# Masked softmax on one core: stores whole and held back, four loads in flight

## The chip, the cores and the metric

The kernel runs on one core of a Trainium2 chip. The metric is the device time of one execution in microseconds (us). The kernel before took 155.86 us, the median of three runs (155.79 to 156.03).

The core has five engines, each with its own queue of instructions: TensorE (PE), VectorE (DVE), ScalarE (ACT), GpSimd (POOL) and SyncE (SP). They wait for one another only through semaphores. Data goes between the chip's main memory (DRAM here) and the on-chip memory SBUF through 16 DMA engines, which all queues share. SBUF has 128 partitions.

## What is computed

A softmax along the last axis of x (16 batches, 8 heads, 256 x 256, float32), where batch b counts only its first lengths[b] columns; the other columns of the result are zero.

```python
def reference(x, lengths):
    batch, heads, seq_q, seq_k = x.shape
    result = np.zeros_like(x)
    for b in range(batch):
        length = lengths[b]
        masked = x[b, :, :, :length].copy()
        masked = masked - np.max(masked, axis=-1, keepdims=True)
        exp_masked = np.exp(masked)
        result[b, :, :, :length] = exp_masked / np.sum(exp_masked, axis=-1, keepdims=True)
    return result
```

The lengths are drawn between 128 and 255. With the draw used here they are 188, 233, 229, 243, 195, 252, 165, 210, 222, 180, 209, 157, 159, 199, 214, 248.

## The kernel before

One batch is 2048 rows of 256 numbers, 2 MB. It is laid over the 128 partitions so that each partition holds 16 whole rows (nt = 16), 16 KB that also lie together in DRAM. SBUF has room for 8 batches (`xt`, 8 slots); batch b uses slot b % 8.

**Loads.** The first four batches (ahead = 4) are loaded whole by SP at the start: batch 0 in two halves (L109), batches 1 to 3 in one transfer each (L111). Their landing raises `s_ld`: s_ld[0] and s_ld[1] for the halves of batch 0, s_ld[b+1] for batch b. Batches 4 to 15 are loaded by POOL in a loop (L153): it reads the length (L156), and a tree of branches (`pick`, L126) issues the transfer of the smallest sufficient width, 160 to 240 columns in steps of 8, or all 256 (L130). Such a narrow load moves only the left part of each row. What stands in the right part of the slot is old or was set to zero (L149), and the mask covers it. Two loads are in flight: load n waits for load n-2 (`s_sw`, one semaphore for even and one for odd batches, L158) and for the store of batch n-8, whose slot it takes (`s_st`, L159). The first load also waits for s_ld[3], the landing of batch 2 (L152).

**Compute.** For each batch VectorE first masks (L195): columns from the length on get a very large negative number. ScalarE then takes the exponential of each of the 16 rows of a partition, with the row's sum as a side result (L252), in two halves of 8 rows. VectorE divides each half by the sums (L219, L222); the end of a half raises `s_out`. VectorE's order is fixed: for batches 4 and on it is first half of b, mask of b+1, second half of b; for batches 1 to 3 the mask of b+1 comes first.

**Stores.** SP issues the stores (L120), in order of the batches. `parts` (L50) says how a batch is cut: whole for batches 0, 13 and 14, in a half and two quarters for 1 to 7, in two halves for 8 to 12 and 15. A part goes as soon as its half is divided (L117), and the first part of a batch also waits until the store of batch b-2 has landed (L119). The cut sets the size of a packet: a quarter has 4 KB per partition, a half 8 KB, a whole batch 16 KB. `s_st` counts 64 for a batch, 16 for each quarter.

SP's queue thus holds loads of batches 0 to 3 and then all stores. POOL's queue holds the loads of batches 4 to 15. On the DMA side they are two queues: q1 (hardware) for what SP issues, q0 (software) for what POOL issues.

Of the kernel before, what the change touches and what calls it, by code (L numbers as in the profile page):

```python
# [16 lines left out]
POOL = mybir.EngineType.Pool  # L17
# [3 lines left out]
def kernel(  # L21
# [6 lines left out]
    nc = tc.nc  # L28
    P = nc.NUM_PARTITIONS

    batch, heads, seq_q, seq_k = x.shape
    rows = heads * seq_q
    assert rows % P == 0
    nt = rows // P
    half = nt // 2
    quarter = nt // 4

    x_f = x.rearrange("b h q k -> b (h q) k").rearrange("b (p t) k -> b p t k", p=P)
    out_f = out.rearrange("b h q k -> b (h q) k").rearrange("b (p t) k -> b p t k", p=P)

    slots = 8
    ahead = 4
    assert slots - ahead == 4 and batch % slots == 0

    widths = list(range(160, 248, 8))
# [1 line left out]
    mid = seq_k // 2  # L47
    big = 1.0e30

    def parts(b):  # L50


        if b == 0:
            cuts = [0, nt]
        elif b < 8:
            cuts = [0, half, half + quarter, nt]
        elif b < 13 or b == batch - 1:
            cuts = [0, half, nt]
        else:
            cuts = [0, nt]  # L60
        return [slice(i, j) for i, j in zip(cuts, cuts[1:])]

    pool = ctx.enter_context(tc.tile_pool(name="all", bufs=1))
    psum = ctx.enter_context(tc.tile_pool(name="psum", bufs=1, space=bass.MemoryType.PSUM))
    xt = pool.tile([P, slots, nt, seq_k], F32, name="xt")
# [11 lines left out]
    seed = pool.tile([1, 2], F32, name="seed")  # L77

    sem = lambda n: ctx.enter_context(nc.semaphore(n))
    s_st = [sem("s_st0"), sem("s_st1")]  # L80
    with tc.tile_critical(no_gpsimd_drain=True):  # L81
# [3 lines left out]
        s_lenf = sem("s_lenf")  # L85
        s_ld = [sem(f"s_ld{k}") for k in range(ahead + 1)]

        s_sw = [sem("s_sw0"), sem("s_sw1")]

        s_iota = sem("s_iota")  # L90
        s_fill = sem("s_fill")
# [2 lines left out]
        s_exp = sem("s_exp")  # L94
        s_out = sem("s_out")

        def length(engine, at):

            return nc.values_load(  # L99
                at,  # L100
                engines=[engine],
                skip_runtime_bounds_check_because="compared with constants, never an address",
            )
# [3 lines left out]
        for h in range(2):  # L107
            s = slice(h * half, (h + 1) * half)
# [1 line left out]
        for b in range(1, ahead):  # L110
            nc.sync.dma_start(out=xt[:, b], in_=x_f[b]).then_inc(s_ld[b + 1], 16)  # L111

        nc.sync.wait_ge(s_exp, 3)
        for b in range(batch):
            s_b = s_st[b % 2]
            for s in parts(b):
                nc.sync.wait_ge(s_out, 2 * b + (s.stop - 1) // half + 1)  # L117
                if b >= 2 and s.start == 0:
                    nc.sync.wait_ge(s_b, 64 * (b // 2 + 1))  # L119
                nc.sync.dma_start(  # L120
                    out=out_f[b, :, s, :], in_=xt[:, b % slots, s, :]
                ).then_inc(s_b, 16 * ((s.stop - s.start) // quarter))

        def pick(v, n, slot, par, ws):  # L126

            if len(ws) == 1:
                w = ws[0]
                nc.gpsimd.dma_start(  # L130
                    out=xt[:, slot, :, :w], in_=x_n[:, n, :, :w]
                ).then_inc(s_sw[par], 16)
                return
            m = (len(ws) - 1) // 2
            with nc.gpsimd.If(v <= ws[m]):  # L135
                pick(v, n, slot, par, ws[: m + 1])
            with nc.gpsimd.Else():
                pick(v, n, slot, par, ws[m + 1 :])

        x_n = x_f.rearrange("b p t c -> p b t c")  # L140
        nc.gpsimd.iota(  # L141
# [1 line left out]
        ).then_inc(s_iota, 1)  # L143
        nc.gpsimd.memset(ones, 1.0).then_inc(s_ones, 1)  # L144
        for par in range(2):
            nc.gpsimd.memset(seed[:, par : par + 1], 0.0).then_inc(s_st[par], 64)  # L146
        nc.gpsimd.wait_ge(s_v, 2)
        for b in range(ahead, slots):
            nc.gpsimd.memset(xt[:, b, :, low:], 0.0).then_inc(s_fill, 1)  # L149
        nc.gpsimd.wait_ge(s_word, 16)  # L150
        nc.gpsimd.wait_ge(s_fill, slots - ahead)
        nc.gpsimd.wait_ge(s_ld[ahead - 1], 16)  # L152
        with nc.Fori(0, (batch - ahead) // 2, 1, engines=[POOL]) as q:  # L153
            for par in range(2):
                n = 2 * q + (ahead + par)
                v_len = length(POOL, word[0:1, bass.ds(2 * n, 1)])  # L156
                with nc.gpsimd.If(q >= 1):
                    nc.gpsimd.wait_ge(s_sw[par], 16 * q)  # L158
                    nc.gpsimd.wait_ge(s_st[par], 64 * q)  # L159
                pick(v_len, bass.ds(n, 1), bass.ds(n % slots, 1), par, widths + [seq_k])  # L160


        nc.tensor.wait_ge(s_ones, 1)
# [4 lines left out]
        v = 0  # L168

        def step(ins):  # L170
# [8 lines left out]
                out=down, in0=iota_i, scalar1=0.5, scalar2=-big, op0=ALU.add, op1=ALU.mult  # L179
# [7 lines left out]
                out=len_s, in0=len_f, scalar1=big, scalar2=None, op0=ALU.mult  # L187
# [4 lines left out]
        def clip(b, s, lo, hi):  # L192

            t = xt[:, b % slots, s, lo:hi]
            return nc.vector.scalar_tensor_tensor(  # L195
                out=t,
                in0=down[:, None, lo:hi].to_broadcast([P, s.stop - s.start, hi - lo]),
                scalar=len_s[:, b : b + 1],
                in1=t,
                op0=ALU.add,  # L200
                op1=ALU.min,
            )

        def mask(b, s):
            v_len = length(DVE, word[0:1, 2 * b : 2 * b + 1])
            if b == 0:
                nc.vector.wait_ge(s_ld[s.start // half], 16)
            elif b < ahead:
                nc.vector.wait_ge(s_ld[b + 1], 16)
            else:  # L210
                nc.vector.wait_ge(s_sw[b % 2], 16 * ((b - ahead) // 2 + 1))
            with nc.vector.If(v_len < mid):  # L212
                clip(b, s, 0, mid)
            clip(b, s, mid, seq_k).then_inc(s_min, (s.stop - s.start) // half)

        def divide(b, h):
# [10 lines left out]
            ).then_inc(s_out, 1)  # L227

        mask(0, slice(0, half))
        mask(0, slice(half, nt))  # L230
        for b in range(batch):


            first = b == 0 or b >= ahead
            if first:
                divide(b, 0)
            if b + 1 < batch:
                mask(b + 1, slice(0, nt))
            if not first:
                divide(b, 0)  # L240
            divide(b, 1)
# [5 lines left out]
        with nc.Fori(0, 2 * batch, 1, engines=[ACT]) as i:  # L247
            nc.scalar.wait_ge(s_min, i + 1)
            at = bass.ds(i % (2 * slots), 1)
            for j in range(half):  # L250
                e = x_h[:, at, j, :]
                ins = nc.scalar.activation(  # L252
                    out=e, in_=e, func=EXP, accum_out=sum_h[:, bass.ds(i, 1), j]
# [3 lines left out]

    with tc.tile_critical(no_gpsimd_drain=True):
        for par in range(2):
            nc.sync.wait_ge(s_st[par], 64 * (batch // 2 + 1))  # L260


# [28 lines left out]
```

## Time and profile before

| | |
|---|---|
| median of three runs | 155.86 us |
| span of the profiled execution | 154.7 us |
| VectorE busy | 115.7 us (75%) |
| ScalarE busy | 105.2 us (68%) |
| GpSimd busy | 19.0 us (12%) |
| read from DRAM | 28.51 MB |
| written to DRAM | 33.55 MB |
| mean DMA rate over the span | 401 GB/s |
| divide of half a batch (L222) | 32 x 2292 ns |
| masks (L195) | 17 instructions, 37.8 us |
| load issued by POOL to its landing | 13.3 to 20.5 us |
| stores issued by SP | 36: 14 of 512 KB, 19 of 1 MB, 3 of 2 MB |

The span is what the profile shows of one execution; the time of a run is a little longer. "Busy" adds up an engine's own instructions. In the strips of the page the span is cut into 40 equal slices of 3.87 us, and a digit is the busy share of a slice in tenths. In the listing of DMA queues the columns are packets, MB, and the time that the packets took as a share of 16 engines over the stretch. A line of waits says which engine's line waited for what: us in total, times, longest. A line in order of time gives the start, the duration, the engine, the line and what it writes and reads; the number in brackets is the idle time just before.

### The profile page before, as it was taken

To read this page: it belongs to the slowest core of one execution; us is meant where nothing else is said; L and a number is where in the kernel's file an instruction comes from. 1 tells how busy PE (TensorE), PEld (TensorE's weight loads), DVE (VectorE), ACT (ScalarE), POOL (GpSimd) and SP (SyncE) were. 2 spreads that over 40 slices of the span, in tenths; PEclk is the share of its full clock that TensorE was granted. 3 is DMA by queue.
4 is the path that set the end of the run, shared out by engine and by line. 5 is a ranking of instruction groups with operands and counts; after the bars stand their busy time and mean duration, and the time that the engine had idled before them with its cause. 6 is when DMAs were issued, how large, how long until landed. Compare 5 with 4: busy or idle time off the path is not lost.

```text
span 154.7 us, 1324 instructions
## 1 busy us (share of the span) xinstructions
PE 0.2 (0%) x1; PEld 0.1 (0%) x1; DVE 115.7 (75%) x84; ACT 105.2 (68%) x514; POOL 19.0 (12%) x25
## 2 busy tenths in 40 slices
PE   0000000000000000000000000000000000000000
PEld 0000000000000000000000000000000000000000
DVE  1249999952999696979979696969689629796700
ACT  3087799992692959778695959595976906959200
POOL 4910031000220110201111020202001000000000
DMA  4999999999999999999999999999999999999992
GB/s 116 426 449 424 428 398 406 398 407 447 400 410 395 402 409 414 415 417 411 404 424 407 417 408 409 415 416 416 416 417 419 419 448 415 426 445 419 430 421 85
DMA packets 9988, 62.08 MB, mean 401 GB/s; under 512 B 850, under 2 KB 946, under 8 KB 6274
## 3 DMA queue, kind: packets, MB, share of 16 engines
q1 hardware_dynamic: 5904, 41.95, 65.8%
q0 software_dynamic: 4080, 20.12, 32.1%
q14 instruction: 2, 0.02, 0.0%
q10 hardware_dynamic: 2, 0.00, 0.0%
HBM read 28.51 MB, written 33.55 MB: 401 GB/s over the span
## 4 chain that ended last, share of the span: by engine, by line
DMA 55%; DVE 19%; ACT 8%; issue 8%; ACTq 2%; SPq 1%; POOLq 1%; DVEq 0%
DMA xt<-in_x_dram 34%; DMA out_dram<-xt 21%; DVE xt L222 9%; DVE xt L195 9%; ACT xt L252 8%; ACTq L252 2%; DVE inv_sum L219 1%; SPq L109 1%; POOLq L99 0%; SPq L111 0%; SPq L120 0%; DVEq L212 0%; POOLq L135 0%; POOLq L130 0%; ACTq L247 0%
## 5 line engine op out<-in xcount | busy, mean ns | idle before, releaser
L252 ACT ACTIVATE xt<-xt x256 | 102.4, 401 | 37.2 <-DVE xt L195 37.2
L222 DVE TENSOR_TENSOR xt<-xt,inv_sum 128x2048 f32<-128x2048 f32 x32 | 73.4, 2292 | 1.1
L252 ACT ACTIVATION_READ_ACCUMULATOR xt<-xt x256 | 47.9, 187 | 0.0
L195 DVE SCALAR_TENSOR_TENSOR xt<-down,len_s,xt 128x2048 f32<-128x2048 f32 (+1 forms) x17 | 37.8, 2222 | 13.1 <-DMA xt<-in_x_dram 13.0
L130 POOL DMA_DIRECT2D xt<-in_x_dram x12 | 12.8, 1064 | 95.5 <-issue 50.6
L219 DVE RECIPROCAL inv_sum<-row_sum 128x8 f32<-128x8 f32 x32 | 6.3, 198 | 14.4 <-ACT xt L252 14.4
L149 POOL MEMSET xt<- 128x1536 f32 x4 | 5.3, 1386 | 1.1 <-DVE len_s L186 1.1
L244 ACT ACT_TABLE_LOAD x1 | 1.3, 1283 | 1.6 <-SPq L81 1.6
L178 DVE TENSOR_SCALAR down<-iota_i 128x256 f32<-128x256 int32 x1 | 0.3, 297 | 1.6 <-POOL iota_i L141 1.6
L183 DVE CAST len_b<-word 1x16 bf16<-1x16 int32 x1 | 0.2, 163 | 0.4 <-DMA word<-in_lengths_dram 0.4
L186 DVE TENSOR_SCALAR len_s<-len_f 128x16 f32<-128x16 f32 x1 | 0.2, 174 | 0.3 <-PE len_f L165 0.3
L141 POOL IOTA iota_i<- 128x256 int32 x1 | 0.3, 331 | 0.6 <-SPq L81 0.6
L146 POOL MEMSET seed<- 1x1 f32 x2 | 0.3, 162 | 0.0
L244 ACT ACTIVATE warm<-const-float32-0.0 128x1 f32<-128x1 f32 x1 | 0.2, 203 | 0.0
L144 POOL MEMSET ones<- 1x128 bf16 x1 | 0.2, 194 | 0.0
L165 PE MATMUL len_f<-len_b,ones 1*128 1x16 bf16 x1 | 0.2, 164 | 2.6 <-DVE len_b L183 2.6
L275 POOL MEMSET const-float32-0.0<- 128x1 f32 x1 | 0.1, 98 | 0.3 <-issue 0.3
L165 PEld LDWEIGHTS len_f<-len_b,ones 1*128 1x128 bf16 x1 | 0.1, 99 | 2.6 <-POOL ones L144 2.6
L275 POOL MEMSET const-float32-1.0<- 128x1 f32 x1 | 0.1, 98 | 0.0
L275 POOL MEMSET const-bfloat16-1.0<- 128x1 bf16 x1 | 0.1, 98 | 0.0
L275 POOL MEMSET const-uint8-127<- 128x1 uint8 x1 | 0.1, 98 | 0.0
L275 POOL BASE_LOAD x1 | 0.0, 17 | 0.1
## 6 DMA issues: line engine op xcount, KB each, us to landing
out_dram<-xt SPq DMA_DIRECT2D x19, 1024.0 KB
out_dram<-xt SPq DMA_DIRECT2D x14, 512.0 KB
xt<-in_x_dram SPq DMA_DIRECT2D x3, 2048.0 KB, 16.1
out_dram<-xt SPq DMA_DIRECT2D x3, 2048.0 KB
xt<-in_x_dram POOLq DMA_DIRECT2D x3, 1728.0 KB, 16.9
xt<-in_x_dram POOLq DMA_DIRECT2D x2, 2048.0 KB, 18.5
xt<-in_x_dram POOLq DMA_DIRECT2D x2, 1600.0 KB, 16.8
xt<-in_x_dram POOLq DMA_DIRECT2D x2, 1280.0 KB, 14.8
```

The costliest lines, as they stand in the source:

```text
L109: nc.sync.dma_start(out=xt[:, 0, s], in_=x_f[0, :, s]).then_inc(s_ld[h], 16)
L130: nc.gpsimd.dma_start(out=xt[:, slot, :, :w], in_=x_n[:, n, :, :w]).then_inc(s_sw[par], 16)
L141: nc.gpsimd.iota(iota_i, pattern=[[1, seq_k]], base=0, channel_multiplier=0).then_inc(s_iota, 1)
L146: nc.gpsimd.memset(seed[:, par : par + 1], 0.0).then_inc(s_st[par], 64)
L149: nc.gpsimd.memset(xt[:, b, :, low:], 0.0).then_inc(s_fill, 1)
L165: nc.tensor.matmul(len_f, lhsT=ones, rhs=len_b, start=True, stop=True).then_inc(s_lenf, 1)
L195: return nc.vector.scalar_tensor_tensor(out=t, in0=down[:, None, lo:hi].to_broadcast([P, s.stop - s.start, hi - lo]), scalar=len_s[:, b : ...
L219: step(nc.vector.reciprocal(out=inv_sum[:, b, s], in_=row_sum[:, b, s]))
L222: nc.vector.tensor_tensor(out=t, in0=t, in1=inv_sum[:, b, s, None].to_broadcast([P, half, seq_k]), op=ALU.mult,).then_inc(s_out, 1)
L244: nc.scalar.activation(out=warm, in_=nc.const_aps.tensor(0.0, (P, 1), F32), func=EXP)
L252: ins = nc.scalar.activation(out=e, in_=e, func=EXP, accum_out=sum_h[:, bass.ds(i, 1), j])
L275: nc = _bacc.Bacc("TRN2", target_bir_lowering=False, num_devices=1)
```

## The change

Every batch is stored whole, in one transfer with 16 KB per partition; `parts` is gone. The store of batch b waits for both halves of its batch, for the store of batch b-2, and, up to batch 11, for the landing of the load of batch b+4. `s_st` counts 16 for a batch.

POOL's loads have four semaphores (lead = 4) in place of two. Load n waits for load n-4 and for the store of batch n-8. The loop runs three times over four loads. The first load waits for s_ld[2], the landing of batch 1; this wait stands inside the loop under a branch that only the first turn takes. SP's wait for the third half's exponential (L113) is gone. VectorE's mask waits on the new semaphores; its instructions and those of ScalarE are the same and in the same order.

```diff
-    def parts(b):
-
-
-        if b == 0:
-            cuts = [0, nt]
-        elif b < 8:
-            cuts = [0, half, half + quarter, nt]
-        elif b < 13 or b == batch - 1:
-            cuts = [0, half, nt]
-        else:
-            cuts = [0, nt]
-        return [slice(i, j) for i, j in zip(cuts, cuts[1:])]
+    lead = 4
+    waves = (batch - ahead) // lead
+    assert waves * lead == batch - ahead
...
-        s_sw = [sem("s_sw0"), sem("s_sw1")]
+        s_sw = [sem(f"s_sw{k}") for k in range(lead)]
...
-        nc.sync.wait_ge(s_exp, 3)
         for b in range(batch):
             s_b = s_st[b % 2]
-            for s in parts(b):
-                nc.sync.wait_ge(s_out, 2 * b + (s.stop - 1) // half + 1)
-                if b >= 2 and s.start == 0:
-                    nc.sync.wait_ge(s_b, 64 * (b // 2 + 1))
-                nc.sync.dma_start(
-                    out=out_f[b, :, s, :], in_=xt[:, b % slots, s, :]
-                ).then_inc(s_b, 16 * ((s.stop - s.start) // quarter))
+            nc.sync.wait_ge(s_out, 2 * b + 2)
+            if b + lead < batch:
+                nc.sync.wait_ge(s_sw[b % lead], 16 * (b // lead + 1))
+            if b >= 2:
+                nc.sync.wait_ge(s_b, 16 * (b // 2 + 1))
+            nc.sync.dma_start(out=out_f[b], in_=xt[:, b % slots]).then_inc(s_b, 16)
...
-            nc.gpsimd.memset(seed[:, par : par + 1], 0.0).then_inc(s_st[par], 64)
+            nc.gpsimd.memset(seed[:, par : par + 1], 0.0).then_inc(s_st[par], 16)
...
-        nc.gpsimd.wait_ge(s_ld[ahead - 1], 16)
-        with nc.Fori(0, (batch - ahead) // 2, 1, engines=[POOL]) as q:
-            for par in range(2):
-                n = 2 * q + (ahead + par)
+        with nc.Fori(0, waves, 1, engines=[POOL]) as q:
+            for k in range(lead):
+                n = lead * q + (ahead + k)
                 v_len = length(POOL, word[0:1, bass.ds(2 * n, 1)])
+                if k == 0:
+                    with nc.gpsimd.If(q < 1):
+                        nc.gpsimd.wait_ge(s_ld[2], 16)
                 with nc.gpsimd.If(q >= 1):
-                    nc.gpsimd.wait_ge(s_sw[par], 16 * q)
-                    nc.gpsimd.wait_ge(s_st[par], 64 * q)
-                pick(v_len, bass.ds(n, 1), bass.ds(n % slots, 1), par, widths + [seq_k])
+                    nc.gpsimd.wait_ge(s_sw[k], 16 * q)
+                    nc.gpsimd.wait_ge(s_st[k % 2], 32 * q + 16 * (k // 2))
+                pick(v_len, bass.ds(n, 1), bass.ds(n % slots, 1), k, widths + [seq_k])
...
-                nc.vector.wait_ge(s_sw[b % 2], 16 * ((b - ahead) // 2 + 1))
+                k = b - ahead
+                nc.vector.wait_ge(s_sw[k % lead], 16 * (k // lead + 1))
...
-            nc.sync.wait_ge(s_st[par], 64 * (batch // 2 + 1))
+            nc.sync.wait_ge(s_st[par], 16 * (batch // 2 + 1))
```

More of the change, by code (lines that the diff above doesn't have):

```diff
@@ L35 @@
     half = nt // 2
-    quarter = nt // 4
     x_f = x.rearrange("b h q k -> b (h q) k").rearrange("b (p t) k -> b p t k", p=P)
@@ L111, with pick @@
             nc.sync.dma_start(out=xt[:, b], in_=x_f[b]).then_inc(s_ld[b + 1], 16)
-        nc.sync.wait_ge(s_exp, 3)
         for b in range(batch):
             s_b = s_st[b % 2]
-            for s in parts(b):
-                nc.sync.wait_ge(s_out, 2 * b + (s.stop - 1) // half + 1)
-                if b >= 2 and s.start == 0:
-                    nc.sync.wait_ge(s_b, 64 * (b // 2 + 1))
-                nc.sync.dma_start(
-                    out=out_f[b, :, s, :], in_=xt[:, b % slots, s, :]
-                ).then_inc(s_b, 16 * ((s.stop - s.start) // quarter))
-        def pick(v, n, slot, par, ws):
+            nc.sync.wait_ge(s_out, 2 * b + 2)
[4 more added lines that the diff above has]
+            nc.sync.dma_start(out=out_f[b], in_=xt[:, b % slots]).then_inc(s_b, 16)
+        def pick(v, n, slot, k, ws):
             if len(ws) == 1:
@@ L131, in pick @@
                     out=xt[:, slot, :, :w], in_=x_n[:, n, :, :w]
-                ).then_inc(s_sw[par], 16)
+                ).then_inc(s_sw[k], 16)
                 return
@@ L135, in pick @@
             with nc.gpsimd.If(v <= ws[m]):
-                pick(v, n, slot, par, ws[: m + 1])
+                pick(v, n, slot, k, ws[: m + 1])
             with nc.gpsimd.Else():
-                pick(v, n, slot, par, ws[m + 1 :])
+                pick(v, n, slot, k, ws[m + 1 :])
         x_n = x_f.rearrange("b p t c -> p b t c")
```

## The prediction

> **What bounds the kernel now.** I read the page first, then the waits of the engines and of SP's queue, then what the DMA queues carried in chosen stretches, and last VectorE in order of time. In the page, the strip of DMA shares and the two data queues:
>
> ```profile
> span 154.7 us, 1324 instructions
> DMA  4999999999999999999999999999999999999992
> q1 hardware_dynamic: 5904, 41.95, 65.8%
> q0 software_dynamic: 4080, 20.12, 32.1%
> ```
>
> The 16 DMA engines are full from the second slice to the last but one. 65.8% + 32.1% = 97.9% of 154.7 us is 151.5 us of packets per engine; the 3.2 us that are left lie before the first packet (first load issued at 1.13 us) and after the last. The chain that ended last also hops from transfer to transfer. So the time is the packet time of one DMA engine plus 3.2 us, as long as it never runs dry, and compute is a second bound below it:
>
> ```profile
> DVE xt L195 <- DMA xt<-in_x_dram: 13.0, 5, 4.4
> ...
> SPq L119 <- DMA out_dram<-xt: 92.3, 14, 9.7
> ```
>
> VectorE waited 13.0 us for loads; SP's queue waited 92.3 us for earlier stores: finished batches lay ready and had no DMA. The price of a packet comes from stretches in which q1 carries stores of one size (columns: packets, MB, share of 16 engines). In this order: 16 KB alone (139 to 146.5 us), 8 KB beside narrow loads (112 to 125), 8 KB alone (148 to 150.5), 4 KB beside narrow loads (74.3 to 78.2 and 93.1 to 96.4):
>
> ```profile
> q1 hardware_dynamic: 217, 3.19, 99.5%
> ...
> q1 hardware_dynamic: 486, 3.49, 64.4%
> q0 software_dynamic: 483, 1.97, 37.7%
> ...
> q1 hardware_dynamic: 147, 1.07, 101.6%
> ...
> q1 hardware_dynamic: 221, 0.85, 54.6%
> ...
> q1 hardware_dynamic: 192, 0.71, 54.1%
> ```
>
> Share times 16 times the stretch, over MB, is engine time per MB: 0.995x16x7.5/3.19 = 37.4 us; 0.644x16x13/3.49 = 38.4; 1.016x16x2.5/1.07 = 38.0; 4 KB 40.1 (0.546x16x3.9/0.85) and 40.2. Narrow loads: 0.377x16x13/1.97 = 39.8. The small semaphore packets are in these figures.
>
> **The change part by part.**
>
> 1. Stores whole. Taken away: 14 stores of 512 KB (7.34 MB), 19 of 1 MB (19.92 MB) and 3 of 2 MB (6.29 MB), in 4, 8 and 16 KB packets: 7.34x40.1 + 19.92x38.4 + 6.29x37.4 = 294 + 765 + 235 = 1294 us of engine time, 80.9 us on each of 16. Added: 33.55 MB in 16 KB packets, 33.55x37.4/16 = 78.4 us. Gain 2.5 us. A 16 KB store beside narrow loads is not seen undisturbed. The 8 KB rows show a surcharge of 38.4 over 38.0, 1%; on the 11 stores that can meet loads (23.07 MB) that is 23.07x37.4x0.01/16 = 0.6 us, so 1.9 at the low end. A worse bound, the stretch from 21 to 28 us, is a rival below. I take 2.2 us, midway. SP also issues 20 instructions fewer (374 ns each), hidden under its 92.3 us of waiting.
>
> 2. Holding store b for load b+4 moves bytes and adds none. SP's queue holds only stores at that point, so behind the wait stand later stores, and behind those POOL's loads (load n waits for store n-8). Store 0, issued at 19.86 us, must now wait for load 4. What fills DMA from 19.9 on: loads 2 and 3 are in flight until about 24 (3.3 + the 20.6 us that the slowest of L111's loads took), and load 4 must follow them. POOL is now released by batch 1, which landed at 2.05 + 11.7 = 13.8 us, instead of batch 2. Before, 18.66 to 20.85 us lay between landing and issue, so load 4 is issued at about 16.1. From there to the first packets can be slow: of the load issued at 20.85 only 0.09 MB had moved by 28 us:
>
> ```profile
> DMA packets 194, 2.69 MB, mean 384 GB/s; under 512 B 16, under 2 KB 16, under 8 KB 35
> ...
> q1 hardware_dynamic: 174, 2.59, 94.6%
> q0 software_dynamic: 19, 0.09, 3.2%
> ```
>
> 19 packets on 16 engines mean a start near 27, a lag of some 6 us. So load 4 flows from about 22, before 24: cost zero, and 2 us of cover. Loads 5 to 7 follow at the 3.2 us between POOL's first two issues (20.85 and 24.04), under 4 us of engine time each. Load 4 (1.64 MB, 39.8x1.64/16 = 4.1 us) lands near 28, against 37.4 before (20.85 + 16.54).
>
> 3. Four loads in flight. By the waits, a load is issued when a store ends and a store when a load lands: four transfers are always under way, each batch a load and a store in turn. One batch is 151.5/16 = 9.5 us of engine time. A turn's dead time is 2.2 + 6 us for a load and 0.4 + 1.4 for a store (first load: issued 1.13, first piece of transfer in the chain at 2.51), 10 us. Four batches give 4x9.5 = 38 us of work per turn; 9.5 + 10 of it is a batch's own, so 18 us of queueing cover the dead time. Cost zero; without this cover each microsecond of dry queue is one of span. POOL runs one more branch (on q) in each turn of its loop, three in all, under the same cover.
>
> 4. Compute. Its rows do not change: per batch two L222 of 2.29, one L195 of 2.35, steps of 8.4 us when not starved. What ends the run after the last load (the mask of batch 15 and its last divide):
>
> ```profile
> 134.97 2.34 DVE L195 SCALAR_TENSOR_TENSOR xt<-down,len_s,xt 128x2048 f32<-128x2048 f32 x1
> ...
> 144.33 2.29 DVE L222 TENSOR_TENSOR xt<-xt,inv_sum 128x2048 f32<-128x2048 f32 x1
> ```
>
> Mask 15 to the last divide's end is 11.7 us. The last store used to leave as two halves; whole, it needs 0.4 + 1.4 + 2.10x37.4/16 = 6.7 us after it. So compute alone ends DMA at mask 15 + 18.4 us. DMA's own end will be near 153.4 - 2.2 = 151.2, so mask 15 must start by 132.8. It will: when load 15 lands, the hold lets at most stores 0 to 10 have moved, with all loads 28.51 + 23.07 = 51.6 of 62.1 MB. At the even pace of 151 us for all, that is 2.6 + 0.83x151 = 128 us. By VectorE's own pace: mask 4 started at 37.62 after 4.42 us idle, now 33.2; 9.6 us to mask 5 (47.21) as before, then ten steps of 8.4 (126.58 to 134.97 is one): 126.8. The later, 128, leaves 4.8 us. Hence the tail costs nothing; without the hold it would (the second rival).
>
> Sum: 154.7 - 2.2 = 152.5 us of profiled span. The profiled execution stands 1.2 us below the median of 155.86, so 155.86 - 2.2 = 153.66; I say 153.6.
>
> **The rivals.**
>
> Slower: 16 KB packets are slow beside the software queue. In the stretch 21 to 28 us, the only one where a 16 KB store meets POOL's loads, q1 took 0.946x16x7/2.59 = 40.9 us per MB, not 37.4. If all 23.07 MB of stores 0 to 10 pay that, +3.5x23.07/16 = 5.0 us, net 2.8 slower than before: 158.7. It decides from 37.4 + 2.5x16/23.07 = 39.1 us per MB on. For it: that row. Against: nearly no narrow data moved there, the whole loads of that stretch were hit as well, it began with POOL's very first issue, and a 16 KB load beside 8 KB stores (127 to 133 us) takes 0.6x16x6/1.54 = 37.4:
>
> ```profile
> q0 software_dynamic: 108, 1.54, 60.0%
> q1 hardware_dynamic: 140, 1.02, 40.1%
> ```
>
> I read it as a start-up cost that stays, moved. Chance 0.10.
>
> No change: loads are starved by big store packets. With 8 KB stores the loads' share was 37.7 to 64.4; packets alternate, some 4.4 KB (1.97 MB in 483 packets, the small ones off) at 39.8 us per MB, 175 ns, to 8 KB at 38.4, 315 ns. Against 613 ns they get 22% while stores are queued. If load 15 then comes as late as before, mask 15 at 134.97 gives DMA's end at 153.4 and a time of 155.9; each microsecond past that costs one. Against it: the hold empties the store queue whenever loads fall behind. Chance 0.06.
> The Trainium skill (DMA: Bandwidth & Descriptors, section "Queues, rings and completion order") says that each engine goes round its queues and changes only at the end of a packet; by it, bigger store packets take from the loads. The 37.7 to 64.4 of the trace agrees with it.
>
> A dry queue. If the lag of load 4 is 10 us and not 6, DMA stands from 24 to 26, and a slow first turn may add as much: 2 to 4 us, 155.6 to 157.6. For it: the slow first load. Against: the 2 us of cover, and the 18 in part 3. Chance 0.06.
>
> The change not doing what it says: POOL may not get four loads out at once, as the trace never shows more than two. Then the third simply follows the first's landing, the queue is still fed, and the time is the forecast's.
>
> **How the numbers follow.** Forecast 0.75, rivals 0.10, 0.06, 0.06, and 0.03 for what I do not see. The forecast's own range is 152.4 to 154.6 (a gain of 3.5 to 1.3, for the rounding of the rows, 0.7% on the smallest, and a little dry time). The range of 8 in 10 goes on to 156.4 to take in the no-change rival and the short dry queue. A measurement here tells a difference from none at about 0.2%, 0.3 us. Faster: 0.75 and 0.03 from mild rivals, 0.78; same 0.07; slower 0.15.
>
> **What would show it.** Right: 16 stores of 2048 KB; the two queues' shares sum to near 149.3 us; DMA strip full throughout; 37.4 to 37.8 us per MB of store beside loads; SP's queue waiting for loads; load 4 landing near 28, the wait of 4.42 at batch 4 gone; mask 15 near 128 or before. Wrong: slices of DMA below 9 around 24 to 30 us or at the end (dry); 39 us per MB or more (slow packets); mask 15 past 133 with VectorE waiting for loads (starved).

## The result and the profile after

The changed kernel takes 158.58 us (158.54 to 158.68, 4 runs) against 155.92 for the kernel before in the same runs: slower by 1.6%, ratio 1.0159 with a 95% interval of 1.0144 to 1.0174. The forecast was 153.6 us, in a range of 152.4 to 156.4.

The page of the profile after, with span, DMA strip and data queues (packets, MB, share of 16 engines over the span):

```profile
span 157.1 us, 1298 instructions
DMA  4999999999999999999999999999999999999991
GB/s 115 434 436 434 432 391 358 434 362 414 415 407 365 413 422 421 394 318 416 428 425 387 406 419 421 421 332 421 402 427 449 417 442 421 430 438 417 438 426 67
q1 hardware_dynamic: 3024, 41.94, 63.4%
q0 software_dynamic: 4080, 20.12, 34.1%
```

DMA is still full in every slice but the first and the last, so nothing ran dry for long. But in five slices the rate falls to 318 to 365 GB/s. In the kernel before it was 395 or more in all but the first and the last:

```profile
GB/s 116 426 449 424 428 398 406 398 407 447 400 410 395 402 409 414 415 417 411 404 424 407 417 408 409 415 416 416 416 417 419 419 448 415 426 445 419 430 421 85
```

By queue, in engine time: q1 (whole loads and stores) went from 65.8% of 154.7 to 63.4% of 157.1, 101.8 to 99.6 us: 2.2 us less, the gain that was forecast. q0 (the narrow loads) went from 32.1% of 154.7 to 34.1% of 157.1, 49.7 to 53.6 us: 3.9 us more for the same bytes in the same packets. That is +1.7 us of the +2.4 us of span; the other 0.7 us is, by the same shares, time outside the packets (3.2 us before, 3.9 now).

Where q0 became dearer shows in what the queues carried in short stretches of the changed kernel. In this order: 25 to 28 us, 68 to 71, 85 to 88, and for comparison 60 to 63, and 126 to 146 for stores by themselves:

```profile
q0 software_dynamic: 201, 1.15, 107.5%
...
q0 software_dynamic: 250, 0.98, 102.3%
...
q0 software_dynamic: 266, 1.09, 101.5%
...
q1 hardware_dynamic: 62, 1.02, 79.3%
q0 software_dynamic: 62, 0.26, 21.5%
...
q1 hardware_dynamic: 587, 8.57, 100.2%
```

In the first three no store moves, and narrow loads have the DMA to themselves. They cost 1.075x16x3/1.15 = 44.9 us of engine time per MB, then 50.1 and 44.7 (25 to 28 us holds some packets of the wide load 5 too, which are cheaper). A share can pass 100% where packets overlap or reach over an edge; by bytes alone the three moved 382, 328 and 362 GB/s, the fourth 426. From 60 to 63 us stores run beside them: 0.215x16x3/0.26 = 39.7, the price of the trace before. The stores cost 37.3 there and 37.4 alone. The fourth stretch also shows how the queues share: 62 packets each.
The Trainium skill (DMA: Bandwidth & Descriptors, section "Queues, rings and completion order") has the engines go round the queues packet by packet; the 62 to 62 agrees.

Counted in slices of 1 us, 11.15 of the 20.12 MB of loads moved in slices in which q1 had less than 15% of the engines, at 44.5 us per MB; the rest cost 40.0. That is 11.15x4.5/16 = 3.1 of the 3.9 us. In the kernel before there is one such slice, with 0.33 MB.

VectorE at batch 4 and at batch 15, and its and SP's waits:

```profile
33.59 2.34 DVE L183 SCALAR_TENSOR_TENSOR xt<-down,len_s,xt 128x2048 f32<-128x2048 f32 x1
...
130.51 2.35 DVE L183 SCALAR_TENSOR_TENSOR xt<-down,len_s,xt 128x2048 f32<-128x2048 f32 x1
```

```profile
DVE xt L183 <- DMA xt<-in_x_dram: 8.6, 5, 3.6
...
SPq L109 <- DMA xt<-in_x_dram: 88.3, 10, 13.8
SPq L107 <- DMA xt<-in_x_dram: 31.5, 2, 25.8
```

Batch 4 no longer waits (4.42 us before), mask 15 starts at 130.5 in place of 135.0, and SP waits for loads, which is the hold (L107; L109 is the next wait, and the list names what came last). The schedule thus did what was worked out, and the price of a narrow load did not stay what it was.

### The profile page after: what moved, and what is told of

Same layout as the page of the kernel before. It is cut to its first block, busy times and chain, and to the rows that moved or that the text cites. A ratio compares the mean times of both kernels' runs of the same rounds, so it can differ in the third digit from the quotient of the medians.

```text
span 157.1 us, 1298 instructions
## 1 busy us (share of the span) xinstructions
PE 0.2 (0%) x1; PEld 0.1 (0%) x1; DVE 115.6 (74%) x84; ACT 105.2 (67%) x514; POOL 19.0 (12%) x25
## 3 DMA queue, kind: packets, MB, share of 16 engines
q1 hardware_dynamic: 3024, 41.94, 63.4%
q0 software_dynamic: 4080, 20.12, 34.1%
## 4 chain that ended last, share of the span: by engine, by line
DMA 71%; issue 6%; DVE 5%; ACT 4%; POOLq 2%; ACTq 1%; SPq 1%; POOL 0%; DVEq 0%
DMA xt<-in_x_dram 57%; DMA out_dram<-xt 14%; ACT xt L241 4%; DVE xt L183 3%; DVE xt L211 2%; ACTq L241 1%; SPq L99 1%; POOLq L121 0%; POOLq L116 0%; POOL xt L116 0%; POOLq L89 0%; DVE inv_sum L208 0%; POOLq L145 0%; POOLq L123 0%; ACTq L236 0%
## 5 line engine op out<-in xcount | busy, mean ns | idle before, releaser
L241 ACT ACTIVATE xt<-xt x256 | 102.3, 401 | 32.8 <-DVE xt L183 32.8
L183 DVE SCALAR_TENSOR_TENSOR xt<-down,len_s,xt 128x2048 f32<-128x2048 f32 (+1 forms) x17 | 37.8, 2222 | 8.7 <-DMA xt<-in_x_dram 8.6
## 6 DMA issues: line engine op xcount, KB each, us to landing
xt<-in_x_dram SPq DMA_DIRECT2D x3, 2048.0 KB, 16.1
```

The lines of the kernel that those rows point to most:

```text
L183: return nc.vector.scalar_tensor_tensor(out=t, in0=down[:, None, lo:hi].to_broadcast([P, s.stop - s.start, hi - lo]), scalar=len_s[:, b : ...
L241: ins = nc.scalar.activation(out=e, in_=e, func=EXP, accum_out=sum_h[:, bass.ds(i, 1), j])
```

## The experiments

Ratios are to the kernel before in the same runs, with 95% intervals. "q0" is the software queue's time per engine, its share times the span. The last column is what q0 moved without stores: MB in slices of 1 us in which q1 had less than 15% of the engines.

| run | stores | hold | loads in flight, released by | time us | ratio | q0 us | without stores, MB |
|---|---|---|---|---|---|---|---|
| before | cut | no | 2, batch 2 | 155.92 | 1 | 49.7 | 0.3 |
| changed | whole | yes | 4, batch 1 | 158.58 | 1.0159 (1.0144 to 1.0174) | 53.6 | 11.2 |
| e1_no_hold | whole | no | 4, batch 1 | 162.38 | 1.0408 (1.0391 to 1.0426) | 53.0 | 8.2 |
| e2_two_loads | whole | yes | 2, batch 1 | 158.86 | 1.0183 (1.0166 to 1.0200) | 54.1 | 13.6 |
| f2_whole_before | whole | no | 2, batch 2 | 162.24 | 1.0405 (1.0377 to 1.0432) | 53.8 | 9.6 |
| f1_halves_held | halves | yes | 4, batch 1 | 157.11 | 1.0059 (1.0043 to 1.0075) | 51.3 | 5.3 |
| f5_cuts_held | cut | yes | 4, batch 1 | 156.38 | 1.0016 (1.0006 to 1.0026) | 50.6 | 3.5 |
| f4_early_four | cut | no | 4, batch 1 | 157.03 | 1.0056 (1.0036 to 1.0076) | 50.0 | 0 |
| g4_four_late | cut | no | 4, batch 2 | 156.54 | 1.0033 (1.0018 to 1.0047) | 49.7 | 0 |
| g3_before_held | cut | yes | 2, batch 2 | 157.45 | 1.0096 (1.0072 to 1.0119) | 51.5 | 4.2 |

**Without the hold.** `e1_no_hold`:

```diff
-            if b + lead < batch:
-                nc.sync.wait_ge(s_sw[b % lead], 16 * (b // lead + 1))
```

> The changed kernel without the wait of store b for load b+4. In the changed kernel a narrow load cost 46 us of engine time per MB in stretches where no store was queued (68 to 71 us: 0.98 MB, 102.3% of 16 engines x 3 us, is 50) and 40 beside stores. Theory A (a narrow load alone in the DMA is slow, and the hold makes such stretches): without the hold stores are queued nearly always, the software queue's time falls from 53.6 us per engine (34.1% of 157.1) to about 50, and the packet time of both queues to 149.5 us; but the loads lose their lead, so mask 15 starts at 134 us or later and the time is 155 to 158. Theory B (four loads in the software queue at once are slow, whatever else runs): the queue's time stays near 53.6 us also beside stores, time 158 or more. Theory C (the waits let DMA run dry, prices do not matter): software queue's time stays at 53 to 54 us.

It took 162.38 us, and q0 stayed at 32.8% of 161.6 us, 53.0. Theory A missed twice: the stretches without stores do not need the hold, and the time was worse than its range. From 84 to 87 us of this run only loads moved, at 1.027x16x3/1.04 = 47.4 us per MB:

```profile
q0 software_dynamic: 266, 1.04, 102.7%
```

By its numbers the run fits theories B and C; the next runs are against them. What the hold had been worth is seen at the end, in VectorE's waits, its mask of batch 15 and the DMA strip of this run:

```profile
DVE xt L181 <- DMA xt<-in_x_dram: 19.9, 10, 4.9
...
142.45 2.35 DVE L181 SCALAR_TENSOR_TENSOR xt<-down,len_s,xt 128x2048 f32<-128x2048 f32 x1 [1.23 <-DMA xt<-in_x_dram]
```

```profile
DMA  4999999999999999999999999999999999974774
```

Mask 15 starts at 142.5, and the DMA stands partly idle in the last slices while compute catches up. Loads starved by big store packets, which the prediction had as a rival, are real; the hold is what keeps them off.

**Two loads in flight.** `e2_two_loads`; a load waits for the load two before it:

```diff
...
-                    nc.gpsimd.wait_ge(s_sw[k], 16 * q)
+                    nc.gpsimd.wait_ge(s_sw[(k + 2) % lead], 16 * q + 16 * (k // 2))
```

> The changed kernel, hold kept, but a load also waits for the load two before it, so that two are in flight as in the kernel before. Theory A: the hold still leaves stretches without stores, narrow loads there still cost 45 us per MB or more, the software queue keeps 52 us per engine or more, time 157 to 160. Theory B: with two in flight the price is 40 everywhere, the software queue's time is 50 us per engine, time 154 to 155.5.

It took 158.86 us with q0 at 54.1: the changed kernel over again. Four loads in flight are not what costs (theory B falls).

**Full loads.** `e3_wide_held` is the changed kernel, `e4_wide_before` the kernel before, both with 256 columns in every load:

```diff
-                pick(..., widths + [seq_k])
+                pick(..., [seq_k])
```

> The changed kernel with every load at the full 256 columns: 16 KB packets in the loads too, 25.17 MB in place of 20.12 from the software queue. At 37.4 us per MB that is 58.8 us per engine, 5.2 more than the 53.6 of the changed kernel and 9.1 more than the 49.7 of the kernel before. Theory A: 16 KB packets do not care whether they are alone, so the loss is gone and only the cheaper stores remain: 158.6 + 5.2 = 163.8 or a little under, 1 to 2.5 us faster than the kernel before with full loads. Theory B and C: the order of the two stays as it was, this one slower by 1 to 3 us than the kernel before with full loads.

> The kernel before with every load at the full 256 columns: 9.1 us more of packet time, so 155.9 + 9.1 = 165.0 us by all theories (its share of loads beside 4 and 8 KB stores grows, which may let the last load land earlier). It is the base for the run before.

They took 164.75 and 165.95 us (ratios to before 1.0561, 1.0544 to 1.0579, and 1.0635, 1.0615 to 1.0656). Each took about 1 us more than expected. With loads in 16 KB packets the changed schedule wins by 1.2 us, about half of the 2.2 that had been forecast. The waits are the same here, so the loss belongs to the narrow loads, and not to the waits. What is missing of the gain is on q0, 60.0 us in e3 and 59.0 in e4. It shows in e3 from 30 to 33.5 us, around the start of the first store, where 0.82 MB of full loads took 84.8% of the engines, 57.9 us per MB. From 27 to 30 us, also without stores, they cost 37.7; what happens at 30 stays open.

**Only part of the change.** Whole stores alone on the kernel before (`f2_whole_before`: `parts` gives `[0, nt]` for every batch); halves in place of whole stores in the changed kernel (`f1_halves_held`); the old cuts in the changed kernel (`f5_cuts_held`); the same without the hold (`f4_early_four`). The core of f1:

```diff
-            nc.sync.dma_start(out=out_f[b], in_=xt[:, b % slots]).then_inc(s_b, 16)
+            for h in range(2):
+                s = slice(h * half, (h + 1) * half)
...
+                nc.sync.dma_start(
+                    out=out_f[b, :, s, :], in_=xt[:, b % slots, s, :]
+                ).then_inc(s_b, 16)
```

> The kernel before with whole stores and nothing else: no hold, two loads in flight. Theory A: the 16 KB packets alone make the stretches without stores; narrow loads 43 us per MB or more, and the last mask comes later than 135 us for want of the hold: 159 to 163. Theory D: no hold, no loss; the cheaper stores show, 153.5 to 155.

> The changed kernel with each store in two halves of 8 KB packets, hold and four loads in flight kept. Theory A now in this form: what decides is whether store packets last beside the loads. A batch needs 54 parts of store to 46 of load; with 16 KB packets stores take 78% while they are queued, run out, and leave narrow loads alone at 46 us per MB; with 8 KB they take 64%, so fewer loads run alone. Expected: narrow loads in all 40 to 42 us per MB (43.7 in the changed kernel), stores 38.4 (37.7), packet time 99.6 + 2 and 53.6 - 2 to 4, time 155.5 to 158. Theory D (the hold itself costs, since it waits for the slowest of the 16 engines): the time stays at 158.6 or goes up by the 2 us of the smaller packets, 160.5.

> The kernel before with its cuts of the stores and no hold, but four loads in flight, released by batch 1. By theory A nothing changes in the packets (stores of 4 and 8 KB still last beside the loads): narrow loads 40 us per MB, time 155 to 156.5. By theory B (four in flight cost) it would be 157 or more.

> The changed kernel with the old cuts of the stores (halves and quarters), hold and four loads in flight kept. Theory A: with 4 KB packets stores take 48% while loads are queued and the hold is what runs them dry, little; narrow loads at 40 to 41.5, stores at 38.6, time 155 to 157. Theory D: 157.5 to 160.

f1, f2 and f5 fell into theory A's ranges of time; f2's narrow loads, at 42.8 us per MB, lie just below its 43. f4 did not: 157.03 is above its 156.5 and just inside theory B's range, though its narrow loads show no loss (q0 50.0); g4 below takes this up. f2 gives the main finding: whole stores by themselves put q0 at 53.8 us and the time at 162.2. Taken in steps, the 3.9 us on q0 are 0.3 for the early release with four loads (f4), 0.6 for the hold (f5), and 3.0 for whole stores (f5 to the changed kernel), read from one profile each. With the hold and four loads kept, q0 falls with the store packet: 53.6 whole, 51.3 in halves, 50.6 with the old cuts; the time with it, 158.6, 157.1, 156.4. Over all rows of the table q0 goes with the last column: 49.7 to 50.0 us where it is near nothing, 50.6 to 51.5 at 3.5 to 5.3 MB, 53.0 to 54.1 at 8.2 to 13.6 MB. Theory D, that the hold costs by its waiting, does not fit f1 and f5.

The arithmetic behind it: a batch is 2.10 MB of store and on average 1.78 MB of load. Packets alternate, so 4 KB store packets against some 4.4 KB load packets keep both queues supplied; 16 KB stores take 79% (above), finish, and leave the loads alone. The odd mixture of halves and quarters in the kernel before had this effect: the stores' share, 54% in the stretches with 4 KB packets and 64% with 8 KB, lies about the 54 of 100 that a batch needs.

**Some loads full.** `g1_wide_from_208`: the changed kernel with `widths[:6] + [seq_k]`, so that loads over 200 columns take all 256.

> The changed kernel, where a load that needs more than 200 columns takes all 256 (6 of 12 loads, 1.21 MB more in all). Packets of 16 KB then meet packets of 16 KB, so stores last beside these loads, and alone they cost 37 to 38 us per MB. Theory A: 8.78 MB of narrow loads at 41 to 44 and 12.58 MB at 37.5 give 52 to 53.6 us per engine in the software queue in place of 53.6, although more bytes move; time 156.8 to 158.3. Theory D (the hold's waiting for the slowest engine): the bytes add 1.21 x 37.5 / 16 = 2.8 us, 160 or more.

It took 158.41 us (1.0150, 1.0124 to 1.0176), 0.1 above theory A's range; q0 was 33.9% of 156.5, 53.1 us, inside it. 1.25 MB more were moved (21.37 against 20.12) for no time, where the price of 37.5 would have been 2.9 us.

**The hold and the number of loads on the kernel before.** `g3_before_held`, `g4_four_late` (f4 with `s_ld[3]` for `s_ld[2]`), `g6_held_late_whole` (g3 with `b < 11` for `b < 13` in `parts`). The core of g3:

```diff
+                if s.start == 0 and b + ahead < batch:
+                    nc.sync.wait_ge(s_sw[b % 2], 16 * (b // 2 + 1))
```

> The kernel before with the hold of store b for load b+4 as its only change (cuts, two loads in flight and the release by batch 2 kept). Theory A: with 4 and 8 KB stores little load runs alone, narrow loads 40 to 41 us per MB, time 155.5 to 156.8. Theory D: the hold costs by itself, 157.5 or more.

> The kernel before with four loads in flight, but released by batch 2 as before. With the release by batch 1 this took 157.0. If the early release is what cost that 0.9 us (the first loads and the first store all within 20 to 28 us, two slices at 360 GB/s), the time is 155.7 to 156.3; if it is the four loads in flight, 156.7 to 157.2.

> The kernel before with the hold, and stores 11 to 14 whole: with the hold the last load lands before store 11 starts, so these four meet no loads and their 16 KB packets should cost 37.4 us per MB, not 38.0 to 38.4, without leaving loads alone. Gain over the run before it: 2 x 2.10 x 0.8 / 16 = 0.2 us. If it beats the kernel before, then by no more than 0.5 us.

g3 took 157.45 us, outside theory A's range and next to theory D's 157.5. Its stretch from 18 to 30 us says why (by engine, then DMA share and GB/s, in steps of 2 us; two of them):

```profile
22.00:24.00 2.00, 0.00 (x0) 0.00 (x0) 1.97 (x3) 2.00 (x11) 0.79 (x2) 1.00 0.67 145
24.00:26.00 2.00, 0.00 (x0) 0.00 (x0) 2.00 (x1) 2.00 (x11) 0.00 (x0) 1.00 0.93 346
```

Store 0 is held and load 4 is released late, so the DMA has too little to do for 2 us, and then load 4 runs alone. This is the dry queue of the prediction's rivals, and here the hold does cost by its waiting. In f5, with the earlier release and four loads, the same two steps have shares of 0.93 and 1.03, and the time is 156.38; which of the two prevents it was not tried apart. g4 took 156.54, between the two cases of its expectation. That is 0.5 us below f4, but the intervals of the two ratios overlap, so the cost of the early release is not resolved. The rest of g4's 0.3% need not be the four loads either: f4 and g4 are built from the changed kernel, without SP's wait for the third half's exponential, and their store 0 starts at 18.6 and 18.7 us in place of 19.9. g6 took 157.50 (1.0088, 1.0066 to 1.0110): no gain from late whole stores was resolved. No run beat the kernel before.

**What makes a narrow load slow.** Being the only queue with work was one reading of all this; the other, that reads of part rows are slow unless stores run beside them. `h1_loads_alone` holds stores 0 to 3 for load 7, so that loads 4 to 7 run alone from 24 to 42 us. `h2_reads_beside` adds 12 reads of 512 KB in 4 KB packets, `h3_writes_beside` 12 writes of the same size, `h4_big_reads_beside` the same bytes in reads with 16 KB packets. The first three lines are h1's and stand in all four; then come the cores of h2 and of h3:

```diff
-                nc.sync.wait_ge(s_sw[b % lead], 16 * (b // lead + 1))
+                k = max(b, lead - 1)
+                nc.sync.wait_ge(s_sw[k % lead], 16 * (k // lead + 1))
...
+        for i in range(12):
+            s = slice(i % 4 * 4, i % 4 * 4 + 4)
+            nc.sync.dma_start(out=spare[:, 4 * i : 4 * i + 4], in_=x_f[1, :, s]).then_inc(s_spare, 16)
...
+            nc.sync.dma_start(out=scratch[i], in_=spare).then_inc(s_spare, 16)
```

> The changed kernel, but stores 0 to 3 are held until load 7 has landed, so that the narrow loads 4, 6 and 7 run from about 25 to 41 us with nothing beside them. Theory A: 45 to 48 us of engine time per MB in that stretch. It is the base for the next run. Time 159 to 162.

> The run before with company of another kind: behind its whole loads SP issues 12 extra loads of 512 KB in 4 KB packets (6.29 MB read from x into a spare tile that nothing uses). Theory A (a narrow load is slow when its queue is the only one with work, whatever the other would carry): in the stretch in which these reads run beside loads 4, 6 and 7 the narrow loads cost 40 us per MB. Theory E (it is the missing writes: reads alone are slow in the memory): they still cost 45 to 48. The time is longer by up to 6.29 x 40 / 16 = 15.7 us and says nothing here.

> As the run with reads beside, but the 12 transfers of 512 KB in 4 KB packets are writes, from a spare tile of zeros to a scratch tensor in DRAM that nothing uses. In the run with 4 KB reads beside, load 4 cost 44.8 us per MB (46 to 48 alone) and load 6 54 (52 to 57 alone), so company as such does not help. Theory E (it is reads that get in the way of reads): beside writes load 4 costs 39 to 40.5 and load 6 39 to 42. Theory F (only the company of big packets helps): they cost 44 or more, as beside 4 KB reads. The time, about 175 us, says nothing.

> As the run with reads beside, but the same 6.29 MB are read in 3 transfers with 16 KB packets, so that narrow loads are only some 22% of what is read at any time. Theory E in its simple form (all reads, so slow): load 4 44 to 48, load 6 50 to 57. Theory F, or E with the share of part rows among the reads as the measure: 39 to 41 for both. The time, about 175 us, says nothing.

Their times were 163.65, 175.40, 172.83 and 178.04 us; the prices are what counts. h1's time is above its 159 to 162. Load 4 (rows of 800 B) in h1 from 24 to 26.5 us, load 6 (672 B) from 34 to 36, and load 7 (864 B) from 38 to 41:

```profile
q0 software_dynamic: 178, 0.85, 101.0%
...
q0 software_dynamic: 123, 0.58, 102.9%
...
q0 software_dynamic: 255, 1.09, 102.1%
```

Loads 4 and 6 beside 4 KB reads (h2, 25 to 29 and 38 to 42 us):

```profile
q0 software_dynamic: 172, 0.83, 57.8%
q1 hardware_dynamic: 171, 0.63, 42.7%
...
q0 software_dynamic: 158, 0.74, 62.6%
q1 hardware_dynamic: 157, 0.57, 39.5%
```

Beside 4 KB writes (h3, 25 to 28 and 37.5 to 42 us):

```profile
q0 software_dynamic: 146, 0.70, 57.4%
q1 hardware_dynamic: 145, 0.53, 43.3%
...
q0 software_dynamic: 217, 0.98, 57.5%
q1 hardware_dynamic: 216, 0.78, 44.7%
```

Load 4 beside 16 KB reads (h4, 24 to 34 us; load 6 there came after the extra reads had ended):

```profile
q1 hardware_dynamic: 208, 3.11, 77.9%
q0 software_dynamic: 203, 0.97, 24.6%
```

| us per MB of engine time | load 4, 800 B rows | load 6, 672 B rows | load 7, 864 B rows |
|---|---|---|---|
| alone (h1) | 47.5 | 56.8 | 45.0 |
| beside 4 KB reads (h2) | 44.6 | 54.1 | 43.9 |
| beside 4 KB writes (h3) | 39.4 | 42.2 | 39.6 |
| beside 16 KB reads (h4) | 40.6 | not seen | not seen |

Each is the share times 16 times the stretch, over the MB (load 7 in h2 from 45 to 51 us, 1.25 MB at 57.1%, and in h3 from 44 to 50, 1.34 MB at 55.3%). Alone, load 6 is far above theory A's 45 to 48. h2 and h3 differ in the direction of the company (and in the tensors used for it: h2 reads batch 1 over and over), and that decides: reads beside reads stay slow, writes beside them bring the price back. So theory A in the form "alone" falls; it holds in the form "no stores beside them". In h4 the loads cost little more than beside writes, but the 16 KB reads cost 0.779x16x10/3.11 = 40.1 in place of 37.4: the loss has moved to them. Apart, the two would take 0.97x47.5 + 3.11x37.4 = 162 us of engine time; together they took 102.5% of 160, 164 us. In h2 nothing is saved either: the 4 KB reads cost 40.2 by themselves (53 to 57 us, 1.63 MB at 102.5%), which gives 0.83x47.5 + 0.63x40.2 = 65 us apart, and 64 together. In h3, with 40.1 for a 4 KB write, it is 0.70x47.5 + 0.53x40.1 = 54.5 us apart and 48.3 together. So in these runs reads beside a narrow load only share its loss, and writes take most of it away. Whether the memory's side or the engines' reading of short rows is the limit was not tried, nor were part rows in SP's queue: every narrow load here comes from the software queue.

## Why the prediction was wrong

*What bounds the kernel.* Right: DMA is full, and the time moved with the packet time, +1.7 of +2.4 us.

*Part 1, whole stores.* This is the step that failed. It gave the stores a new price and left the loads at the "39.8" of the prices; what bigger store packets do to the loads was put at nothing without a reason. For the stores it was right: q1 lost 2.2 us, the value taken. But 16 KB stores take 79% of the engines while they last and then leave the loads without company, at 45 to 50 us per MB in this kernel. On q0 that cost 3.0 us from f5 to the changed kernel, and 4.1 in f2, where whole stores are the only change. The 39.8 was taken for a property of the packet. All rows it came from had stores beside the loads, because the kernel before nearly always has. The step should have asked what company each price was measured in, and bounded it for loads without stores; the trace before has no row of narrow loads by themselves, which was itself the warning. The rival "16 KB packets are slow beside the software queue" gave 158.7, next to the measured time, but by luck: stores beside loads cost 37.3 us per MB (60 to 63 us), not 39.1 or more.

*Part 2, the hold, "moves bytes and adds none".* It failed in the same way, in small: it adds no bytes, but it leaves loads without stores, 0.6 us more on q0 from f4 to f5. The details of this part were right: load 4 was issued at 15.3 us (16.1 forecast) and landed at 29.6 (28), batch 4 did not wait, and the DMA did not run dry at the release; g3 shows that it does with the late release and two loads.

*Part 3, four loads in flight at no cost.* Right in the changed kernel: with two in flight it takes 158.86. On the kernel before, g4 is 0.3% slower, and what of that is the four loads is not resolved.

*Part 4, the tail.* Right: mask 15 at 130.5, 2.3 us inside the limit of 132.8 (4.8 were forecast), and without the hold it is 142.5 and the tail is exposed.

*The rivals.* "Loads starved" weighed the change of shares from 37.7 against 22% only by when the last load lands. The same shares have a second effect, that stores run out first, and that was not worked out. None of the three signs of being wrong that the prediction named came (dry slices, slow store packets, mask 15 past 133); the price of a load was not among them.

## What to carry to other kernels

A price read from a profile holds for the company that it was measured in. Before a change of packet sizes or of order, ask which transfers will then run without the others, and look for a row in which they already do; if there is none, that is the unknown cost to bound. Where two DMA queues alternate packet by packet, the sizes of their packets set the shares; here shares near the ratio of the bytes (54 to 64% for 54 of 100) kept loads and stores running side by side.

## What was not expected of the hardware

Reads of rows of 672 to 864 B, taken out of a pitch of 1024 B, cost 45 to 57 us of engine time per MB without writes beside them, and 39 to 42 with them. Whole rows cost 37.4 beside stores and 37.8 without (h1 from 28 to 31 us, 1.29 MB at 101.7%), but for the stretch of e3 above. Put per row, loads 4, 6 and 7 in h1 took 38.0, 38.2 and 38.9 ns of engine time, and a whole row at 37.4 us per MB takes 38.3 ns: without writes, leaving columns out saved these three loads no time. That is no rule for every length: rows of 640 B moved without stores at 45.2 us per MB, 28.9 ns a row (changed kernel, 88 to 90 us, loads 11 and 12, 0.73 MB at 103.1%).
The Trainium skill (DMA: Bandwidth & Descriptors, section "Specifications") gives 512 B as the least transfer for the full rate. Load 6 with its rows of 672 B moved 0.58 MB in the 2 us shown of h1, 290 GB/s, while stores by themselves moved 8.57 MB in 20 us, 429 GB/s. So here that size is not enough when only loads run; the measurement decides.
